# The kernel product of an SSM mixer, computed on quarters of the matrix engine's columns

## The chip, the cores and the metric

The kernel runs on one core of a Trainium2 chip. The metric is the device time of one execution in microseconds, the median of repeated runs. A core has TensorE (PE in the profile, with its weight loads as PEld), VectorE (DVE), ScalarE (ACT), GpSimd (POOL) and SyncE (SP), each with its own instruction stream that it takes in order, and DMA queues.

## The reference

The program is one inference step of a two-layer streaming encoder on 1024 prompt positions and 64 sample positions, 1088 columns in all, width 1024. Layer 0 mixes tokens by windowed attention, layer 1 by a diagonal state-space model (SSM). Each mixer is followed by a gated ConvFFN of inner width 2816. Only the SSM matters here:

```python
def s5_mixer(h, h0_re, h0_im, lam_re, lam_im, log_dt, b_re, b_im, c_re, c_im, d_skip, w_glu, b_glu):
    ...
    lr, li, bbr, bbi = s5_discretize(lam_re, lam_im, log_dt, b_re, b_im)
    ...
        _, _, sr, si = lax.associative_scan(_affine_combine, (ar, ai, xr, xi), axis=1)
        y = jnp.einsum('blgp,gip->blgi', sr, cr) - jnp.einsum('blgp,gip->blgi', si, ci)
    ...
    y = ys.transpose(1, 0, 2, 3, 4).reshape(b, t, D_MODEL) + d_skip.astype(jnp.float32) * h.astype(jnp.float32)
```

There are 64 groups of 16 channels, each with a complex state of 64 dimensions. The parameters do not depend on the activations, so what follows from them alone can be computed at any time before the SSM layer runs.

## The kernel before, in words

The kernel handles eight positions at a time. Within such a block of eight, the output is a product with a short matrix kernel, K[t] = Re(C A^t B) for t = 0 to 7, of 16 by 16 for each group. Between blocks a scan carries the state, for which the kernel needs the tables B A^s and C A^t and some phase tables. All of these are written to a DRAM array `prm`, from which the SSM stage loads them.

**The preparation.** `ssm_prep` (L1098) is a generator that makes the tables as side work while layer 0's ConvFFN runs its up-projection. It first runs `ssm_small` (L892), which makes the discretised parameters with many small VectorE instructions, and then eight chunks, `ssm_chunk(q)` (L1016) and `ssm_toeplitz(q)` (L1086). A chunk has 8 groups, as 4 pairs; the two groups of a pair lie on partitions 0 to 63 and 64 to 127. In the order of the code a chunk does this:

- VectorE builds `ct`, C A^t for t = 0 to 8, real and imaginary (L1034 to L1039, through two scratch tiles `m`). ScalarE copies it, rearranged, to `oc` (L1042), which SyncE's queue stores to `prm` (L1043).
- ScalarE writes B of the 8 groups into the tile `bd` (L1048). `bd` is zeroed once (L1007) and holds, for each pair g and each of real and imaginary c, a matrix of 128 by 128, in which the pair's 32 columns stand at 32 g and all others are zero.
- VectorE builds `w`, B A^s (L882 to L887, the helper `cmul`).
- TensorE multiplies `bd` by `ct` into the PSUM tile `kps` (L1062): eight matmuls, all accumulated over the whole 128 rows, since the zero columns add nothing to the other pairs. They are in float32, which takes two passes each, so the profile shows 16 a chunk.
- VectorE adds D to K[0] and copies `kps` into `kt` (L1066, L1067). SyncE's queue stores `kt` to `kd` (L1068), from which `ssm_toeplitz` reads it back in eight loads as tile `tl` (L1094). ScalarE copies that to `tp` (L1095), which goes to `prm` (L1096).
- TensorE transposes `w` into two PSUM tiles `wps` (L1073), four transposes for the real part (c = 0) and four for the imaginary part (c = 1). ScalarE copies each into `b3` (L1074), which goes to `prm` (L1075).
- GpSimd makes phase tables `tab` (L1081, shown as L882 to L887 on POOL), which its queue stores (L1084).

**Buffers.** `ct`, `oc`, `w`, `b3`, `tab`, `tl` and `tp` share two buffers (`pt`, L136), so a chunk's tiles wait for one another's stores. `m` has one buffer. `kps` and the `wps` of c = 0 share the PSUM buffer `sm0`; the `wps` of c = 1 uses `sm1`.

**What sets the order.** The tile framework writes each engine's instruction order ahead of the run. Each instruction has a priority, which is its place in the order of tracing, and each engine takes the instruction of lowest priority number among those that the framework holds ready. `later(n)` (L118) shifts that number. The up-projection calls `aside` (L443) after every tile of 128 output features, and `aside` advances the preparation by one `yield` with its numbers shifted later by `LOW` = 1500 (L447). So the side work ranks behind the main work around it, and fills what it leaves free. `order(x, behind)` (L112) adds that a matmul of the chunk may not stand ahead of the last up-projection matmul traced before it (L1059).

**The main work around it.** `up_block` (L401) computes one tile of 128 features for one block of columns (384, 384 and 320): 8 steps in the inner dimension times 3 matmuls (`mm3`, L221 to L225: high and low parts of a split float32) into one of six PSUM buffers `mm`. VectorE multiplies each block by the norm's factors (L411, L413) and does two taps of the convolution (L420, L421), the gate (L437), half of the weights' split (L216) and sums for a later product (L358 to L373, tile `jt`).

Elsewhere in the program, attention computes `po` (L796) in two matmul shapes of 64 columns, one for PSUM partitions 0 to 63 and one for 64 to 127, and the norms transpose a row factor on TensorE (L284).

Of the kernel before, what the change touches and what calls it, by code (L numbers as in the profile page):

```python
# [8 lines left out]
F32 = mybir.dt.float32  # L9
F32R = mybir.dt.float32r  # L10
I32 = mybir.dt.int32
AF = mybir.ActivationFunctionType
# [3 lines left out]
P = 128  # L16
# [9 lines left out]
LOW = 1500  # L26
# [17 lines left out]
class Core:  # L44
# [166 lines left out]
    behind = ()  # L211
# [680 lines left out]
    def ssm_small(self):  # L892

        nc, a = self.nc, self.a
# [5 lines left out]
        sm = self.prep.tile([P, 1024], F32, name="sm0", tag="sm").rearrange("p (a q) -> p a q", a=32)  # L900
# [79 lines left out]
        c, s = cs, sn  # L980
        for k in range(10):
# [8 lines left out]
            c, s = (ph[:, 0, k - 2], ph[:, 1, k - 2]) if k > 1 else (ta[:, 8], ta[:, 9])  # L990
# [3 lines left out]
        for t, n, p0 in ((self.tq[:, :, 0:32], 16, 0), (self.tp[:, :, 18:36], 9, 4)):  # L994
            t = t.rearrange("p q (c k) -> p q c k", c=2)
            V.memset(t[:, :, 0, 0:1], 1.0)
            V.memset(t[:, :, 1, 0:1], 0.0)
            w, k = 1, p0
            while w < n:
# [3 lines left out]
                m = [m[:, i, :NPR * u].rearrange("p (q j) -> p q j", j=u) for i in range(2)]  # L1003
                self.cmul(V, [t[:, :, i, w:w + u] for i in range(2)], [t[:, :, i, 0:u] for i in range(2)], y, m)
                w, k = w + u, k + 1
        self.bd_ = self.prep.tile([P, 4, 2, P], F32, name="bd", tag="sm")
        V.memset(self.bd_, 0.0)  # L1007
        self.dv = self.prep.tile([P, 24], F32, name="dv")
        nc.sync.dma_start(self.dv[:, 16:], a["s_d"])
# [6 lines left out]
    def ssm_chunk(self, q):  # L1016

        nc, a = self.nc, self.a
        G, V = nc.gpsimd, nc.vector
        gs = slice(4 * q, 4 * q + 4)  # L1020
# [8 lines left out]
        ct = self.pt([P, 4, 2, 9, 16], "ct")  # L1029
# [13 lines left out]
        nc.sync.dma_start(self.prm[:, gs, OC:OC + 256], oc.rearrange("p g c i t -> p g (c i t)"))  # L1043

        for e, r in enumerate((slice(0, 64), slice(64, 128))):
            o = self.bd_[r, 0, 0, 16 * e:16 * e + 1]
            o = bass.AP(tensor=o.tensor, offset=o.offset, ap=[o.ap[0], [2 * P + 32, 4], [P, 2], [1, 16]])
            nc.scalar.activation(o, self.tq[r, gs, 32:64].rearrange("p g (c j) -> p g c j", c=2), AF.Copy)  # L1048

        w = self.pt([P, 4, 2, 16, 8], "w")  # L1050
        m = self.pm2()
# [5 lines left out]

        kps = self.sm_ps("kps", 0)
        behind = self.last_mm  # L1059
        for g in range(4):  # L1060
            for c in range(2):
                x = nc.tensor.matmul(kps[:, :P], self.bd_[:, g, c], ct[:, g, c, 0:8].rearrange("p t i -> p (t i)"),  # L1062
                                     start=g + c == 0, stop=g + c == 4)
                self.order(x, behind)
        kt = self.prep.tile([P, P], F32, name="kt")
        V.scalar_tensor_tensor(kt[:, 0:16], self.dv[:, :16], self.dv[:, 16 + q:17 + q], kps[:, 0:16], op0=ALU.mult, op1=ALU.add)  # L1066
        V.tensor_copy(kt[:, 16:], kps[:, 16:P])  # L1067
        nc.sync.dma_start(self.kd[q * P:q * P + P, 7:].rearrange("j t i -> j (t i)"), kt)  # L1068
        b3 = self.pt([P, 4, 2, P], "b3")
        for c in range(2):  # L1070
            wps = self.sm_ps("wps", c)
            for g in range(4):
                self.order(nc.tensor.transpose(wps[:, g * P:g * P + P], w[:, g, c].rearrange("p j s -> p (j s)"), self.ident), behind)  # L1073
            nc.scalar.activation(b3[:, :, c], wps.rearrange("p (g n) -> p g n", g=4), AF.Copy)  # L1074
        nc.sync.dma_start(self.prm[:, gs, OW:OW + 256], b3.rearrange("p g c n -> p g (c n)"))  # L1075

# [523 lines left out]
```

## Time and profile before

| | |
|---|---|
| median of 3 runs | 2255.86 us (2252.57 to 2258.36) |
| the profiled execution, its own time | 2264.88 us |
| its span, first to last instruction | 2263.1 us |
| mean granted TensorE clock | 0.990 |
| up-projection of layer 0 with the SSM preparation | about 402 to 925 us of the span |
| chunks of the preparation (L1007 on) | about 590 to 925 us |
| PE busy from 590 to 925 us | 327.78 of 335 us |
| VectorE busy in the same stretch | 251.28 us |

A row of the timeline has the start, the duration, the engine, the line of the kernel, the operation, out<-in by tile names, the shape and the count, and in brackets the engine's idle time before it with what ended that. `128*128` on a matmul is rows by columns of the weights. Matmuls are pipelined, so their durations overlap, and what one costs is read from start to start. The profile names the helper's line where a helper records the operation, as with L882 to L887 for `cmul`.

### The profile page before, as it was taken

How to read it: one execution, taken by the hardware profiler on the slowest of the kernel's cores; microseconds unless marked ns; L12 is line 12 of the kernel's file. 1: busy time of each engine (PE TensorE's matmuls, PEld its weight loads, DVE VectorE, ACT ScalarE, POOL GpSimd, SP SyncE). 2: the span in 40 equal slices, each digit the busy share in tenths (PEclk: the TensorE clock that was granted, in tenths of full speed). 3: DMA queues.
4: the chain of work that ended last, by engine and by line, in shares of the span. 5: the costliest groups of instructions: out<-in, count | busy, mean ns of one | idle time of the engine just before them, and what ended most of it. 6: DMA issues, size and time to landing. Idle time of an engine off the chain costs nothing. (4 is left out here: it accounts for less than half of the span.)

```text
span 2263.1 us, 36074 instructions
## 1 busy us (share of the span) xinstructions
PE 2201.7 (97%) x13875; PEld 2122.4 (94%) x13875; DVE 1688.5 (75%) x2954; ACT 1019.2 (45%) x1839; POOL 415.2 (18%) x474
## 2 busy tenths in 40 slices
PE   8999999999999999999998899999999999999997
PEld 8987789999999999999996799999999999989997
DVE  8677647989877777667767855588997787686764
ACT  5255747422333343455534641263544444355543
POOL 5322004200042423000200034352011011100000
PEclk9999999999999999999998999999999999999999
DMA  5100014656345565887749888652266577578773
GB/s 195 37 21 29 16 65 151 242 191 211 107 138 185 178 203 179 259 288 222 227 164 339 262 286 300 234 166 74 96 233 218 213 287 258 193 250 278 222 256 99
DMA packets 208124, 428.48 MB, mean 189 GB/s; under 512 B 23312, under 2 KB 114224, under 8 KB 205008
## 3 DMA queue, kind: packets, MB, share of 16 engines
q1 hardware_dynamic: 175648, 326.56, 44.0%
q0 software_dynamic: 23984, 95.12, 11.6%
q10 hardware_dynamic: 8320, 4.49, 0.9%
q8 instruction: 109, 1.79, 0.3%
q14 instruction: 63, 0.52, 0.1%
HBM read 297.75 MB, written 128.37 MB: 188 GB/s over the span
## 5 line engine op out<-in xcount | busy, mean ns | idle before, releaser
L223 PE MATMUL mm<-hl,whl 128*128 128x384 f32 (+1 forms) x1960 | 643.8, 329 | 7.7 <-DVE hl L306 3.1
L225 PE MATMUL mm<-hh,whl 128*128 128x384 f32 (+1 forms) x1960 | 641.1, 328 | 2.3 <-DVE whl L216 2.3
L224 PE MATMUL mm<-hh,whl 128*128 128x384 f32 (+1 forms) x1960 | 642.2, 328 | 0.0
L223 PEld LDWEIGHTS mm<-hl,whl 128*128 128x128 f32 x1960 | 368.4, 188 | 10.8 <-DVE hl L306 4.5
L225 PEld LDWEIGHTS mm<-hh,whl 128*128 128x128 f32 x1960 | 368.4, 188 | 2.9 <-DVE whl L216 2.9
L224 PEld LDWEIGHTS mm<-hh,whl 128*128 128x128 f32 x1960 | 368.7, 188 | 0.0
L216 ACT ACTIVATE whl<-raw 128x1024 fp32r<-128x1024 f32 x202 | 212.9, 1058 | 339.1 <-PE mm L225 176.4
L216 DVE TENSOR_TENSOR whl<-raw,whl 128x1024 fp32r<-128x1024 f32 x202 | 254.4, 1263 | 96.7 <-ACT whl L216 96.2
L223 PE MATMUL mm<-gt,whl 128*128 128x384 f32 (+1 forms) x968 | 318.5, 329 | 7.9 <-DVE y L613 3.6
L225 PE MATMUL mm<-gt,whl 128*128 128x384 f32 (+1 forms) x968 | 316.9, 328 | 0.7 <-DVE whl L216 0.7
L224 PE MATMUL mm<-gt,whl 128*128 128x384 f32 (+1 forms) x968 | 317.3, 328 | 0.0
L223 PEld LDWEIGHTS mm<-gt,whl 128*128 128x128 f32 x968 | 182.9, 189 | 10.5 <-DVE y L613 4.9
L225 PEld LDWEIGHTS mm<-gt,whl 128*128 128x128 f32 x968 | 182.7, 189 | 1.0 <-DVE whl L216 1.0
L224 PEld LDWEIGHTS mm<-gt,whl 128*128 128x128 f32 x968 | 182.8, 189 | 0.0
L194 DVE TENSOR_TENSOR whl<-raw,whl 128x1024 fp32r<-128x1024 f32 x84 | 96.3, 1153 | 73.0 <-ACT whl L193 72.4
L193 ACT ACTIVATE whl<-raw 128x1024 fp32r<-128x1024 f32 x84 | 82.6, 986 | 126.8 <-DMA raw<-sd 51.0
L419 ACT ACTIVATE t<-u,ppt 128x1090 f32<-128x1090 f32 x88 | 114.2, 1298 | 50.6 <-DVE u L521 24.6
L420 DVE SCALAR_TENSOR_TENSOR t<-u,ppt,t 128x1090 f32<-128x1090 f32 x88 | 123.6, 1406 | 9.8 <-ACT t L419 9.1
L421 DVE SCALAR_TENSOR_TENSOR t<-u,ppt,t 128x1090 f32<-128x1090 f32 x88 | 123.4, 1403 | 0.4
L563 DVE TENSOR_TENSOR gt<-gr,gt 128x768 fp32r<-128x768 f32 (+2 forms) x106 | 90.2, 880 | 10.7 <-ACT gt L562 10.1
L331 POOL TENSOR_TENSOR y<-y,xl 128x768 f32<-128x768 f32 (+1 forms) x16 | 31.3, 1954 | 354.0 <-DVE y L328 288.0
L562 ACT ACTIVATE gt<-gr 128x768 fp32r<-128x768 f32 (+2 forms) x106 | 78.3, 771 | 39.5 <-DMA gr<-gd 30.2
(390 smaller groups left out, 4181.0 us busy)
## 6 DMA issues: line engine op xcount, KB each, us to landing
raw<-in_w_up SPq DMA_DIRECT2D x88, 512.0 KB, 4.3
raw<-in_w_down SPq DMA_DIRECT2D x74, 512.0 KB, 4.5
raw<-sd SPq DMA_DIRECT2D x40, 512.0 KB, 4.6
sj<-in_w_up POOLq DMA_DIRECT2D x68, 256.0 KB, 6.4
su<-sj POOLq DMA_DIRECT2D x34, 512.0 KB, 5.8
raw<-su SPq DMA_DIRECT2D x34, 512.0 KB, 4.8
pm<-prm SPq DMA_DIRECT2D x32, 522.0 KB, 8.2
gr<-td SPq DMA_DIRECT2D x40, 384.0 KB, 5.9
```

Of the source, the lines that this page charges most:

```text
L193: nc.scalar.activation(w[:, 0], raw, AF.Copy)
L194: nc.vector.tensor_sub(w[:, 1], raw, w[:, 0].bitcast(F32))
L216: x = nc.scalar.activation(w[:, 0], raw, AF.Copy), nc.vector.tensor_sub(w[:, 1], raw, w[:, 0].bitcast(F32))
L223: nc.tensor.matmul(out, w[:, 0, sl], xl, start=start, stop=False)
L224: nc.tensor.matmul(out, w[:, 0, sl], xh, start=False, stop=False)
L225: self.last_mm = nc.tensor.matmul(out, w[:, 1, sl], xh, start=False, stop=stop)
L331: x = by[q].tensor_add(yq, yq, xs[q])
L419: nc.scalar.activation(t, u[:, 0:T + 2], AF.Identity, bias=cb(m), scale=cw(0, m))
L420: nc.vector.scalar_tensor_tensor(t, u[:, 1:T + 3], cw(1, m), t, op0=ALU.mult, op1=ALU.add)
L421: self.last_conv = nc.vector.scalar_tensor_tensor(t, u[:, 2:T + 4], cw(2, m), t, op0=ALU.mult, op1=ALU.add)
L562: nc.scalar.activation(x[:, 0, u], raw, AF.Copy)
L563: nc.vector.tensor_sub(x[:, 1, u], raw, x[:, 0, u].bitcast(F32))
```

## The change

The tile `bd` is cut to the pair's own 32 columns: each of its 8 matrices is now 128 by 32. The eight products go to four different quarters of PSUM partitions, `kps[32 g : 32 g + 32]`, each accumulated over two matmuls (c = 0 and 1) in place of eight. The loops are swapped, so that four successive matmuls go to four different quarters. The products and the transposes get priority numbers that are 4 x 1500 lower than before. The transposes of the imaginary part (c = 1) are traced ahead of those of the real part.

```diff
-        self.bd_ = self.prep.tile([P, 4, 2, P], F32, name="bd", tag="sm")
+        self.bd_ = self.prep.tile([P, 4, 2, 32], F32, name="bd", tag="sm")
...
         for e, r in enumerate((slice(0, 64), slice(64, 128))):
-            o = self.bd_[r, 0, 0, 16 * e:16 * e + 1]
-            o = bass.AP(tensor=o.tensor, offset=o.offset, ap=[o.ap[0], [2 * P + 32, 4], [P, 2], [1, 16]])
-            nc.scalar.activation(o, self.tq[r, gs, 32:64].rearrange("p g (c j) -> p g c j", c=2), AF.Copy)
+            nc.scalar.activation(self.bd_[r, :, :, 16 * e:16 * e + 16], self.tq[r, gs, 32:64].rearrange("p g (c j) -> p g c j", c=2), AF.Copy)
...
-        for g in range(4):
-            for c in range(2):
-                x = nc.tensor.matmul(kps[:, :P], self.bd_[:, g, c], ct[:, g, c, 0:8].rearrange("p t i -> p (t i)"),
-                                     start=g + c == 0, stop=g + c == 4)
+
+        for c in range(2):
+            for g in range(4):
+                with self.later(-4 * LOW):
+                    x = nc.tensor.matmul(kps[32 * g:32 * g + 32, :P], self.bd_[:, g, c], ct[:, g, c, 0:8].rearrange("p t i -> p (t i)"),
+                                         start=c == 0, stop=c == 1)
                 self.order(x, behind)
...
-        for c in range(2):
+        for c in (1, 0):
             wps = self.sm_ps("wps", c)
             for g in range(4):
-                self.order(nc.tensor.transpose(wps[:, g * P:g * P + P], w[:, g, c].rearrange("p j s -> p (j s)"), self.ident), behind)
+                with self.later(-4 * LOW):
+                    x = nc.tensor.transpose(wps[:, g * P:g * P + P], w[:, g, c].rearrange("p j s -> p (j s)"), self.ident)
+                self.order(x, behind)
```

## The prediction

> **What bounds the kernel now.** I read the page first, for the engine with the least idle time.
>
> ```profile
> PE 2201.7 (97%) x13875; PEld 2122.4 (94%) x13875; DVE 1688.5 (75%) x2954; ACT 1019.2 (45%) x1839; POOL 415.2 (18%) x474
> ```
>
> TensorE (PE) is busy 97% of a 2263.1 us span, so a change pays by the PE time or PE idle time that it takes away. The changed lines run between 590 and 925 us, beside the first ConvFFN's up-projection, so next I asked for the waits of PE in that stretch (total, times, longest) and for its groups of instructions (busy, mean ns, idle before).
>
> ```profile
> PE wps L1073 <- DVE kt L1067: 4.4, 3, 1.7
> PE wps L1073 <- DVE w L887: 2.9, 3, 1.2
> ```
>
> ```profile
> L1062 PE MATMUL kps<-ct,bd 128*128 128x128 f32 x128 | 23.8, 272 | 0.0
> ```
>
> These are all the waits of PE there: six, 7.3 us, all ahead of the transposes. In three of them `kt` had not yet been copied out of `kps` (both use PSUM bank sm0), in three `w` was not finished. The products `kps` have no wait. Durations overlap, so costs have to come from start to start, which the timeline of PE gives.
>
> ```profile
> 617.84 0.38 PE L1062 MATMUL kps<-ct,bd 128*128 128x128 f32 x2
> 617.98 0.39 PE L223 MATMUL mm<-hl,whl 128*128 128x320 f32 x1
> 618.21 0.38 PE L1062 MATMUL kps<-ct,bd 128*128 128x128 f32 x2
> 618.35 0.40 PE L224 MATMUL mm<-hh,whl 128*128 128x320 f32 x1
> 618.58 0.31 PE L225 MATMUL mm<-hh,whl 128*128 128x320 f32 x1
> 618.73 0.30 PE L223 MATMUL mm<-hl,whl 128*128 128x320 f32 x1
> 618.87 0.31 PE L224 MATMUL mm<-hh,whl 128*128 128x320 f32 x1
> ```
>
> One `kps` product (two passes, "x2") and one `mm` of the up-projection alternate. A cycle takes 618.21 - 617.84 = 0.37 us; an `mm` alone takes (618.87 - 618.58) / 2 = 0.145. So a product costs 0.225 us, a pass 0.1125, the eight of a chunk 1.8 us, all eight chunks 14.4 us. That is the most the first half of the change can work on.
>
> **The change part by part.** *Quarter columns.* Each product now fills 32 output columns, so four should run abreast. No 32-column product is in this trace; attention's `po` has 64-column ones, in two halves.
>
> ```profile
> 141.06 0.31 PE L225 MATMUL gq<-hh,whl 128*128 128x320 f32 x1
> 141.30 1.09 PE L796 MATMUL po<-ptT,vt 128*64 128x256 f32 x8
> 142.32 0.44 PE L789 MATMUL tps<-ident,ptT 128*128 128x128 f32 x2
> ```
>
> PE was free for `po` at 141.06 + 0.145 = 141.205 and went on at 142.32: 1.11 us for eight passes of 256 columns. One after the other they would take 8 x 0.225 = 1.8; two abreast 0.9. So they ran two abreast, and going into this shape and out of it cost 0.21. For `kps`: 16 passes on four quarters, 4 x 0.1125 + 0.21 = 0.66 us a chunk in place of 1.8, a gain of 1.14, times eight 9.1 us. Bounds: if only two run abreast, as in the row, 0.9 + 0.21 = 1.11 and a gain of 5.5; if none do, 1.8 + 0.21 and a loss of 1.7. I take 9.1, since the row shows full overlap for as many column groups as its work had.
>
> The weight loads of `po` in the same place:
>
> ```profile
> 141.29 0.64 PEld L796 LDWEIGHTS po<-ptT,vt 128*64 128x64 f32 x8 [0.19 <-issue]
> ```
>
> Eight loads lie within 0.64 us, under the matmuls of 141.30 to 142.39. The Trainium skill, TensorE: Matmul & The Clock Gate, Part 3, says that weight loads overlap matmuls in flight only where the row groups differ; quarters of the columns share all rows, so by that rule the loads would lie bare and the gain be lost. This row disagrees for halves; that it holds for quarters is not shown, and it is a rival below.
>
> *In one run, early.* The products and transposes got priority 1500 later than where they are traced, and now 4500 earlier. Before, PE reached them by priority; that is why they alternate with `mm`, whose numbers run beside theirs. Now they go into PE's order as soon as the schedule holds their inputs ready. For the transposes a run saves nothing:
>
> ```profile
> 620.01 0.27 PE L1073 MATMUL wps<-ident,w 128*128 128x128 f32 x1
> ...
> 620.27 0.27 PE L1073 MATMUL wps<-ident,w 128*128 128x128 f32 x1
> ...
> 621.53 0.34 PE L224 MATMUL mm<-hh,whl 128*128 128x384 f32 x1
> 621.71 0.60 PE L1073 MATMUL wps<-ident,w 128*128 128x128 f32 x4
> 622.07 0.42 PE L225 MATMUL mm<-hh,whl 128*128 128x384 f32 x1
> 622.33 0.34 PE L223 MATMUL mm<-hl,whl 128*128 128x384 f32 x1
> ```
>
> Two `mm` of 384 columns (0.175 each, the step from 622.33 back over the run) and four transposes take 0.80 us, so one is 0.1125; an interleaved one, in a cycle of 0.26 us with an `mm` of 0.145, costs 0.115: no difference.
>
> *The old waits.* With c = 1 first, into bank sm1, and the products well ahead of `w`, the copy of `kt` has the whole building of `w` to finish in. The 4.4 us go. The 2.9 us for `w` go as they stand too, and what may come instead is counted as new, below. Each wait also costs a restart:
>
> ```profile
> 779.87 0.34 PE L223 MATMUL mm<-hl,whl 128*128 128x384 f32 x1
> 781.65 0.63 PE L1073 MATMUL wps<-ident,w 128*128 128x128 f32 x4 [1.44 <-DVE kt L1067]
> ```
>
> From 779.87 to 781.65 is 1.78 us where 0.175 would do: 1.6 lost, 0.16 above the idle time. The six waits are worth 7.3 + 6 x 0.16 = 8.2 us.
>
> *The new waits.* This decides the sign. A run that PE meets early makes every `mm` behind it wait for `ct` (L1039) and `w`, because PE takes its instructions in order. Today the products have room:
>
> ```profile
> 801.81 0.76 DVE L1036 TENSOR_TENSOR ct<-m 128x576 f32<-128x576 f32 x1 [5.02 <-ACT tp L1095]
> 802.48 1.35 DVE L421 SCALAR_TENSOR_TENSOR t<-u,ppt,t 128x1090 f32<-128x1090 f32 x1
> 803.75 0.55 DVE L411 TENSOR_TENSOR u<-rb,mm 128x384 f32<-128x384 f32 x1
> ...
> 806.95 0.75 DVE L1039 SCALAR_TENSOR_TENSOR ct<-m 128x576 f32<-128x576 f32 x1
> ```
>
> `ct` was done at 807.70 and PE met `kps` here:
>
> ```profile
> 796.90 0.34 PE L225 MATMUL mm<-hh,whl 128*128 128x384 f32 x1
> ...
> 813.86 0.38 PE L1062 MATMUL kps<-ct,bd 128*128 128x128 f32 x2
> ```
>
> That is 6.2 us of cover, which the early priority gives away. How late the side work really is can be read from VectorE's (DVE's) order. L1036 was written ahead of the L411 at 803.75, which takes the block that PE closed at 796.90 + 0.34 = 797.24 (counting blocks against L411s). A ready L411 outranks side work, so the schedule held L1036 startable by 797.24; on the chip it started at 801.81, 4.6 us later, held by the load of the Toeplitz tile. Over the chunks:
>
> ```profile
> DVE ct L1036 <- ACT tp L1095: 29.9, 7, 6.2
> DVE w L884 <- DMA prm<-oc: 9.6, 7, 2.8
> ```
>
> 29.9 us in seven waits, 4.3 us each. Against that stands what the schedule allows between an input and a matmul placed at its readiness. The broadcast transposes of the norms (L284) are such, with lower-ranking `mm` all around:
>
> ```profile
> 1545.05 0.16 DVE L291 SCALAR_TENSOR_TENSOR nvsqb<-nvsqb 128x3 f32<-128x3 f32 x1
> ```
>
> ```profile
> 1122.47 0.32 PE L284 MATMUL pr<-ident,nvsqa 128*128 128x128 f32 x1 [0.81 <-DVE nvsqa L291]
> ...
> 1548.89 0.49 PE L284 MATMUL pr<-ident,nvsqb 128*128 128x128 f32 x3
> ```
>
> The input was there 1548.89 - 1545.21 = 3.7 us before PE came in one case and 0.8 us after in another. The second figure already contains a late VectorE, so I take 3.0, near the upper end: new waits of 7 x (4.3 - 3.0) = 9.1 us. Ends: zero, and 29.9 if nothing is allowed. The second row above helps a little: `kps` run early frees the buffer of `ct`, so `w` need not wait for the store of `oc`; that is VectorE's time, hidden behind PE, and priced at nothing. The store of `kd` and the copies to `b3` move with their matmuls on SyncE's and ScalarE's queues, in the same order and number; if a weight load queued behind one of them came late, PE would show a wait for `whl`, of which it now has none in this stretch.
>
> *The smaller `bd`.* One memset of 256 elements a partition instead of 1024, once, on VectorE: nothing.
>
> **The sum.** -9.1 - 8.2 + 9.1 = -8.2 us. The profiled execution took 2264.88 us, 9.0 above the median of 2255.86; the change is the same amount in both, so about 2256.7 if profiled, and 2247.7 by the median. A difference under 0.3%, 6.8 us, can't be told from none here.
>
> **The rivals.** *PE takes over the side work's lateness (slower).* Place: the first `kps` of a chunk, waiting for `ct`. Price: 29.9 us of new waits, so -9.1 - 8.2 + 29.9 = +12.6, 2268.5 us. It decides against the change from 17.3 us of new waits, 2.5 us a chunk, that is once the schedule's allowance is under 1.8. For it: the waits of L1036 are there in all seven chunks. Against: the 3.7 us seen at L284.
>
> *The quarters do not run abreast*, by the rule named above or because the runs are broken up by `mm`. Then +1.7 - 8.2 + 9.1 = +2.6, 2258.5 us. For it: no quarter is in the trace. Against: the `po` rows.
>
> *No new waits.* The side chain has fewer waits of its own (9.6 us on L884 go), and the allowance covers the rest: -17.3, 2238.6 us. Against: six waits exist today with 6 us of cover.
>
> **How the numbers follow.** Forecast 0.45 (its own range 2243 to 2254), slower rival 0.20, quarters not abreast 0.15, no new waits 0.20. The forecast's gain of 8.2 lies just over the 6.8 bound, so it gives 0.25 to faster and 0.20 to same; no new waits is all faster; the quarters give 0.12 to same and 0.03 to slower; the slower rival 0.17 to slower, 0.03 to same. Together 0.45 faster, 0.35 same, 0.20 slower. The range goes from 2238, no new waits, to 2268, the slower rival's price; beyond it lie the lower half of the one and the upper half of the other, 2 in 10.
>
> **What would show it.** `kps` as 128*32, sixteen passes within 0.7 us, no `mm` between; if a chunk's run takes 1 us or more the first term is wrong. No idle time at L1073 for `kt`. A new row of PE waiting at L1062 for `ct`: under 10 us in all bears out the forecast, 20 or more the slower rival. Chunks closer together than today, as PE no longer holds them back; now the eight lie within 615.6 to 893.5 us, some 39 apart:
>
> ```profile
> L1062 PE MATMUL kps<-ct,bd x128: 270/273/275, 615.6 to 893.5; 128*128 128x128 f32 x128
> ```
>
> If the run behaves and the waits are gone, yet the time stays, look for PE waits on `whl` or on `u` in the same stretch.

## The result, and the profile after

| | before | after |
|---|---|---|
| median | 2256.61 us (2252.57 to 2258.36, 4 runs) | 2275.2 us (2272.19 to 2279.82, 4 runs) |
| profiled execution, its own time | 2264.88 us | 2273.9 us |
| its span | 2263.1 us | 2272.1 us |
| mean granted clock in it | 0.990 | 0.986 |

The changed kernel is slower by 0.9%: ratio 1.0087, 95% interval 1.0064 to 1.0109, or 18.6 us by the medians. The forecast was 2247.7 us, its range ended at 2268.

Of the page of the changed kernel, the line of busy times (PE had 2201.7 us, DVE 1688.5 before):

```profile
PE 2201.1 (97%) x13875; PEld 2115.9 (93%) x13875; DVE 1689.7 (74%) x2954; ACT 1018.2 (45%) x1839; POOL 421.2 (19%) x474
```

PE executes as many instructions as before and is busy as long, while the span is 9 us longer; so the loss must be idle time, or work at a slower pace. The waits of PE from 590 to 925 us in the changed kernel (total, times, longest), which were six at the transposes before:

```profile
PE kps L1062 <- DVE ct L1036: 15.5, 7, 5.2
```

The six old waits are gone, seven new ones have come at the products, and they are longer. The products in the view by tile (min/median/max of one in ns, then first and last start), and one chunk's products in the timeline of PE:

```profile
L1062 PE MATMUL kps<-ct,bd x128: 272/297/419, 596.6 to 850.2; 128*32 128x128 f32 x128
```

```profile
596.30 0.33 PE L224 MATMUL mm<-hh,whl 128*128 128x384 f32 x1
596.56 0.43 PE L1062 MATMUL kps<-ct,bd 128*32 128x128 f32 x8
596.91 0.44 PE L225 MATMUL mm<-hh,whl 128*128 128x384 f32 x1
597.19 0.33 PE L223 MATMUL mm<-hl,whl 128*128 128x384 f32 x1
...
598.92 0.34 PE L224 MATMUL mm<-hh,whl 128*128 128x384 f32 x1
599.19 0.43 PE L1062 MATMUL kps<-ct,bd 128*32 128x128 f32 x8
599.55 0.44 PE L225 MATMUL mm<-hh,whl 128*128 128x384 f32 x1
599.83 0.34 PE L223 MATMUL mm<-hl,whl 128*128 128x384 f32 x1
```

The quarters do run abreast, but in two runs of four products (eight passes each), with twelve `mm` between in this chunk and 12 to 30 in the others. The first run (c = 0) needs only the real half of `ct` (L1036), the second the imaginary half (L1039), and the schedule put each where its own input was held ready. From 596.30 to 597.19 is 0.89 us in which two `mm` take 0.35; a run costs 0.54, a chunk 1.1 instead of 1.8.

Now the longest of the waits: first PE, then DVE and ACT in the same microseconds of the changed kernel.

```profile
768.51 0.34 PE L223 MATMUL mm<-hl,whl 128*128 128x384 f32 x1
774.03 0.65 PE L1062 MATMUL kps<-ct,bd 128*32 128x128 f32 x8 [5.18 <-DVE ct L1036]
774.62 0.69 PE L224 MATMUL mm<-hh,whl 128*128 128x384 f32 x1
775.10 0.52 PE L225 MATMUL mm<-hh,whl 128*128 128x384 f32 x1
775.42 0.52 PE L223 MATMUL mm<-hl,whl 128*128 128x384 f32 x1
```

```profile
766.23 0.54 DVE L411 TENSOR_TENSOR u<-rb,mm 128x384 f32<-128x384 f32 x1
773.22 0.76 DVE L1036 TENSOR_TENSOR ct<-m 128x576 f32<-128x576 f32 x1 [6.45 <-ACT tp L1097]
```

```profile
771.27 1.92 ACT L1097 ACTIVATE tp<-tl 128x1024 f32<-128x1024 f32 x1 [13.04 <-DMA gd<-t]
```

Three engines stand in a row: PE waits for `ct`, DVE for the copy `tp<-tl` of the chunk before, and that copy came late. The `mm` behind the wait show a second cost: their starts are 0.32 us apart, not 0.174. The stretch cut into pieces of 3.41 us, with the granted clock in the column after the busy times:

```profile
764.48:767.89 3.41, 3.41 (x23) 3.41 (x22) 2.29 (x4) 0.00 (x0) 0.12 (x1) 1.00 0.88 243
767.89:771.30 3.41, 0.96 (x6) 0.64 (x4) 0.00 (x0) 0.03 (x1) 0.00 (x0) 1.00 0.71 218
771.30:774.71 3.41, 0.68 (x9) 0.30 (x9) 1.46 (x3) 2.83 (x2) 0.00 (x0) 0.50 0.18 63
774.71:778.13 3.42, 3.42 (x11) 3.42 (x12) 3.42 (x8) 2.67 (x5) 0.00 (x0) 0.50 1.04 327
778.13:781.54 3.41, 3.41 (x26) 2.96 (x25) 3.41 (x6) 1.57 (x3) 0.00 (x0) 1.00 0.87 299
```

A piece in which PE was idle for most of the time is followed by a piece at half clock: 11 instructions of PE lie in the fourth, 26 in the fifth.

To compare kernels, I measured in each trace the time from one `mm` at 565 us to another, 1960 `mm` later (before: 565.38 to 919.14, 353.8 us; after: 565.23 to 926.08, 360.9), and split it by the steps from start to start: the `mm` themselves (323.9 us in each, at 0.146 or 0.174 apiece), what products and transposes add, waits over 0.15 us, and what the `mm` take longer at half clock. A product or transpose at half clock takes longer too, and that part is in its own column: without it and the restart behind a wait, the changed kernel's products would cost some 8.9 us instead of 9.9 (16 runs of 0.555) and e4's some 6.2 instead of 8.5 (8 runs of 0.773, as in e6). This is called the stretch below; each row is one execution, the ratio is that of the timed runs. (In an edited kernel a line can stand a few numbers off.)

| kernel | stretch | products | transposes | waits | half clock | ratio of times (95%) |
|---|---|---|---|---|---|---|
| before | 353.8 | 14.3 | 8.4 | 7.2 | 0 | |
| before, profiled again (e12) | 349.5 | 14.3 | 7.9 | 3.5 | 0 | 1.000 (0.999 to 1.001) |
| after | 360.9 | 9.9 | 7.1 | 15.5 | 4.4 | 1.0087 (1.0064 to 1.0109) |
| after, old order of halves (e8) | 363.8 | 10.7 | 7.7 | 16.7 | 4.9 | 1.0062 (1.0046 to 1.0078) |
| e1_no_early | 365.2 | 34.1 | 7.1 | 0 | 0 | 1.0068 (1.0048 to 1.0087) |
| e2_early_only | 374.5 | 16.6 | 7.1 | 18.1 | 8.8 | 1.0089 (1.0072 to 1.0106) |
| e3_run_old_place | 353.1 | 10.4 | 8.0 | 7.7 | 3.1 | 1.002 (1.0006 to 1.0033) |
| e4_imag_first | 362.9 | 8.5 | 7.9 | 17.2 | 5.0 | 1.0051 (1.0035 to 1.0067) |
| e5_swap_only | 356.2 | 14.3 | 10.0 | 6.5 | 1.6 | 1.0008 (0.9996 to 1.002) |
| e6_run_late_transposes | 347.2 | 6.2 | 8.4 | 8.9 | 0 | 1.0032 (1.0019 to 1.0046) |
| e9_full_late_transposes | 360.8 | 14.3 | 9.0 | 10.0 | 3.6 | 1.0066 (1.005 to 1.0081) |
| e10_tiling_swap | 349.0 | 6.2 | 9.1 | 8.4 | 1.6 | 1.0016 (1.0006 to 1.0026) |
| e11_tiling_only | 349.8 | 6.2 | 9.6 | 9.5 | 0.6 | 1.0012 (1.0001 to 1.0022) |
| e13_less_dve | 360.4 | 6.2 | 9.5 | 14.7 | 6.0 | 1.0056 (1.0034 to 1.0079) |
| e14_tiling_no_oc | 349.6 | 6.2 | 8.3 | 8.2 | 3.1 | 0.9991 (0.9978 to 1.0004) |
| e15_after_no_oc | 365.9 | 10.6 | 7.4 | 17.2 | 6.8 | 1.006 (1.0037 to 1.0083) |
| e16_before_no_oc | 348.7 | 14.3 | 7.7 | 2.8 | 0 | 0.9967 (0.9953 to 0.9981) |
| e17_tiling_short_tab | 347.1 | 6.2 | 8.9 | 6.9 | 1.2 | 1.0021 (1.0008 to 1.0033) |
| e18_before_short_tab | 346.7 | 14.3 | 7.7 | 0.9 | 0 | 0.9993 (0.998 to 1.0007) |
| e19_after_short_tab | 351.7 | 9.5 | 7.4 | 9.1 | 1.6 | 0.9994 (0.9979 to 1.0009) |

### The profile page after: what moved, and what is told of

Same layout as the page of the kernel before. It is cut to its first block, busy times and chain, and to the rows that moved or that the text cites. A ratio compares the mean times of both kernels' runs of the same rounds, so it can differ in the third digit from the quotient of the medians.

```text
span 2272.1 us, 36102 instructions
## 1 busy us (share of the span) xinstructions
PE 2201.1 (97%) x13875; PEld 2115.9 (93%) x13875; DVE 1689.7 (74%) x2954; ACT 1018.2 (45%) x1839; POOL 421.2 (19%) x474
## 5 line engine op out<-in xcount | busy, mean ns | idle before, releaser
L223 PEld LDWEIGHTS mm<-hl,whl 128*128 128x128 f32 x1960 | 370.2, 189 | 10.6 <-DVE hl L306 5.8
L411 DVE TENSOR_TENSOR u<-rb,mm 128x384 f32<-128x384 f32 (+1 forms) x164 | 80.3, 501 | 31.9 <-PE mm L225 27.1
```

Of the source, the lines that this page charges most:

```text
L223: nc.tensor.matmul(out, w[:, 0, sl], xl, start=start, stop=False)
L411: nc.vector.tensor_mul(u[:, t0 + 2:t0 + 2 + np_], rb[:, t0:t0 + np_], ps[:, :np_])
```

## The experiments

The theories. **P**: the early place makes the loss, since PE, which takes its instructions in order, waits for `ct`. **Q**: the quarter shape makes it. **D**: the stretch isn't where the time hangs; what is gained or lost there changes behind it.

**e1_no_early.** The changed kernel without the priority, products and transposes both.

```diff
-                with self.later(-4 * LOW):
+                if True:
```

> Quarter columns and the other order of the transposes, but the priority of the products and transposes as before. Theory P (the early place makes PE wait for ct): no PE wait for ct at L1062, the 7 us of waits at the transposes stay. But the products stand alone between matmuls of the up-projection, so each pays for going into the quarter shape and out of it. In the changed kernel a run of four products cost 0.55 us, of which 0.23 is passes, so one alone should cost about 0.5 and the 64 of them 32 us in place of 14.4: 2270 to 2278 us. Rival Q (the quarter shape itself is what costs): slower as well, by the same rows. This run prices the shape; it does not tell the two apart.

Measured: 2272.25 us. The waits in the stretch are gone, all of them (P had expected the 7 us at the transposes to stay), and the time is as bad for another reason. The timeline of PE in this kernel:

```profile
615.62 0.34 PE L225 MATMUL mm<-hh,whl 128*128 128x384 f32 x1
615.88 0.41 PE L1062 MATMUL kps<-ct,bd 128*32 128x128 f32 x2
616.22 0.41 PE L223 MATMUL mm<-hl,whl 128*128 128x320 f32 x1
616.57 0.41 PE L1062 MATMUL kps<-ct,bd 128*32 128x128 f32 x2
```

Products and `mm` alternate. A cycle takes 616.57 - 615.88 = 0.69 us, and less 0.145 for the `mm` a product costs 0.54 instead of 0.225: each change of shape is paid for, in both directions. The eight chunks' products cost 34.1 us instead of 14.3. So the quarters need the run, and the early place was the change's way to get it.

**e2_early_only.** The kernel before, full columns and old loops, with the early priority alone.

```diff
+                with self.later(-4 * LOW):
                     x = nc.tensor.matmul(kps[:, :P], ...
...
+                with self.later(-4 * LOW):
                     x = nc.tensor.transpose(wps[:, g * P:g * P + P], ...
```

> Full columns and the old order of the loops; only the early priority of products and transposes is taken over. Theory P: PE waits at L1062 for ct, 10 to 20 us in all, with half clock after the longest waits; the old waits at the transposes go; nothing is gained on the products: 2262 to 2276 us. Rival Q: without the quarter shape there is nothing to lose, and the old waits go: 2246 to 2256 us.

Measured: 2276.17 us. The waits of PE in the stretch:

```profile
PE kps L1063 <- DVE ct L1036: 18.1, 6, 4.6
```

The early place alone costs as much as the whole change: P holds, and Q isn't needed for the loss. (The place is not quite the same: the schedule put e2's products up to 90 `mm` earlier than the changed kernel's.)

**e3_run_old_place.** The changed kernel with the products at the old place, seven of eight in one run, and the transposes about 20 `mm` behind. (The comments in the cuts of code from here on are added for the reader.)

```diff
-                with self.later(-4 * LOW):    # products
+                with self.later(0):
-                with self.later(-4 * LOW):    # transposes
+                with self.later(20):
```

> Quarter columns, products all at one priority number at the old place, so that seven of the eight stand in one run there, transposes 20 numbers later than that. Theory P: no PE wait for ct, few or none at the transposes, the products some 1.1 us a chunk in place of 1.8: 5 to 6 us gained there and up to 8 at the waits: 2242 to 2250 us. Rival Q: the shape costs as in the changed kernel, 2268 or more. Rival D (what is lost comes after 925 us): 2256 or more, with no waits at the products.

Measured: 2261.67 us. The loss is gone but for 0.2%, which speaks for P and against Q; the gain that P expected isn't there. Its waits:

```profile
PE wps L1074 <- DVE kt L1067: 7.7, 5, 3.2
```

**e4_imag_first.** The changed kernel with the imaginary half first, so that the first product already needs all of `ct`.

```diff
-        for c in range(2):
+        for c in (1, 0):
...
-                                         start=c == 0, stop=c == 1)
+                                         start=c == 1, stop=c == 0)
```

> The changed kernel with the imaginary part first among the products, so that the first of them needs all of ct and the eight stand in one run. Theory P: the waits for ct stay, now for L1039, 8 to 20 us in all; one entry and exit less a chunk gains 0.3 us, 2.6 in all: 2266 to 2278 us. Rival Q: half the entries and exits are gone, so the loss against before should halve: near 2266 us, with the waits no matter.

Measured: 2268.29 us. The eight products stand in one run and cost 8.5 us instead of 9.9 (6.2 instead of 8.9 at full clock), the waits stay: 16.2 us for `ct` (L1039) and 1.1 for `kt`. Two runs or one is a small matter beside the waits.

**e5_swap_only** and **e8_after_no_swap**: the kernel before with the transposes' halves in the new order, and the changed kernel with them in the old order.

```diff
-        for c in range(2):
+        for c in (1, 0):
             wps = self.sm_ps("wps", c)
```

> The kernel before with one edit: the two halves of the transposes in the other order. The first four then stand 4 `mm` behind the last product instead of 9, the second four 12 `mm` further on instead of 7, and nothing goes early. Every theory here expects little: the first four are ready at the same moment as before (they need w, which both halves share) and the waits before them in the kernel before were 7.2 us in the stretch from about 565 to 919 us. Theory P (the early place of the products made the loss): 2252 to 2266 us, the wait for w at the transposes up by at most 5 places x 0.17 us x 8 chunks = 7 us. A rival, that the swap by itself carries the loss: 2272 us or more.

> The changed kernel with the transposes' halves in the old order. With all of them put early the order on TensorE, ScalarE, GpSimd and SyncE is the same as in the changed kernel. Theory P: the same time, 2270 to 2279 us, and the same waits for ct (14 to 18 us) in the stretch from about 565 to 919 us, which would be some 6 to 10 us longer than in the kernel before. The rival, that the swap of the halves carries part of the loss: below 2266 us. D (a part of the loss lies behind that stretch): the milestones behind 930 us are later than the kernel before's by more than this stretch has lost.

Measured: 2258.09 and 2270.27 us. The swap does nothing that can be told from none. e8 stands for a second look at the changed kernel, since the order on PE is the same: its waits for `ct` are 16.7 us, its half clock 4.9.

**e12_before_again.** No edit.

> The kernel before, profiled once more, to see how far one profiled execution of it lies from another, stage by stage. If its first profile (8 us above its median) was long in the last stages only, this one has the same 353 to 355 us in the stretch from about 565 to 919 us and is some 8 us shorter behind 1930 us; the loss of the changed kernel is then 7 to 10 us in the stretch and 8 behind it. If the stretch itself varies, it comes out below 348 us, and the whole loss of the changed kernel lies in the stretch.

Measured: 2254.34 us, span 2251.5. The waits of PE in the stretch were shorter by half than in the first profile:

```profile
PE wps L1073 <- DVE kt L1067: 2.8, 3, 1.4
PE wps L1073 <- DVE w L887: 0.6, 1, 0.6
```

The stretch itself varies, by 4.3 us, and what lies behind it by 7.4 (1344.0 and 1336.6 us from the end of the stretch to the end of the span). The expectation's two cases came half each. With two profiles of either order, the stretch is 351.7 us on average before and 362.4 after, 10.7 more; behind it, 1340.3 and 1342.3 (1346.0 and 1338.5), 2 more. That makes 12.7 us, near the 13.2 of e8's runs and below the 18.6 of the first comparison. D isn't needed for the loss: 10.7 of the 12.7 us lie in the stretch. (Of all twenty profiles, e2 and e15 have the longest stretches and the shortest rest, 1330 us; part of such a loss may come back behind the stretch, but both were also the fastest executions of their kernels, so it can be scatter.)

**e6_run_late_transposes** and **e9_full_late_transposes.** All eight products in one run at the old place, the transposes 17 and some 35 `mm` behind: e6 in quarters, e9 over the full columns, in the same order at every place of PE.

```diff
+                with self.later(0 if g + c else 2):    # products
...
+                with self.later(20 if c else 50):      # transposes, c = 1 first
```

> The quarters, all eight products in one run at the old place, the first transposes about 17 `mm` behind them and the second four 16 to 22 further on. Theory P: the products wait for nothing (at that place they waited for nothing in the kernel before and in e3_run_old_place), the transposes stand some 5 places behind those of e3_run_old_place, whose waits for kt were 7.7 us at five of eight, so these go mostly; without waits the clock is not halved. In the stretch from about 565 to 919 us the products cost 5 to 6 us instead of 14.3, the transposes about 8, the waits 0 to 3 instead of 7.2: 11 to 16 us below the kernel before, 2241 to 2250 us. The rival D (anything that is gained in this stretch is lost again downstream of it, as the place of the products is not what the time hangs on): 2255 us or more, with the stretch itself shorter.

> The same order as in e6_run_late_transposes on every place of TensorE, but the products over all 128 columns into a zero-padded square, as before: the price of the quarters alone, in one run each. P: 8 chunks x (1.8 - 0.66) = 9 us slower than e6_run_late_transposes by the prediction's figures, 2250 to 2259 us. If the quarters gain nothing (their switch costs what they save): the same as e6_run_late_transposes within 3 us.

Measured: 2263.01 and 2271.71 us. A chunk's run in e6:

```profile
615.56 0.31 PE L224 MATMUL mm<-hh,whl 128*128 128x320 f32 x1
615.80 0.64 PE L1062 MATMUL kps<-ct,bd 128*32 128x128 f32 x16
616.37 0.41 PE L225 MATMUL mm<-hh,whl 128*128 128x320 f32 x1
```

Its weight loads, and the same chunk's run in e9:

```profile
615.80 0.38 PEld L1062 LDWEIGHTS kps<-ct,bd 128*32 128x32 f32 x16 [0.19 <-issue]
```

```profile
615.83 0.31 PE L224 MATMUL mm<-hh,whl 128*128 128x320 f32 x1
615.97 1.95 PE L1063 MATMUL kps<-ct,bd 128*128 128x128 f32 x16
617.67 0.39 PE L225 MATMUL mm<-hh,whl 128*128 128x320 f32 x1
```

In e6, from 615.56 to 616.37, less an `mm`, is 0.665 us: the prediction's 0.66 for a chunk, with nothing yet for the slower `mm` behind it; with that, 6.2 us for all eight chunks instead of 14.3. In e9 the same stretch of a chunk, 615.83 to 617.67 less an `mm`, is 1.70 us. At equal order the quarters are worth 8.1 us on PE and 8.7 in time (9 expected), so Q is refuted, and with the opposite sign. But e6 as a whole came out 0.3% slower than the kernel before, where P expected a gain. The order of the two is what costs: e9, with the old full columns in this order, is 0.66% slower than the kernel before, more than the quarters bring. Where e6 loses is not settled: its profiled execution, 2255.4 us, was the fastest of its twelve, and its stretch is 4.5 us shorter than the average of before, so the result is what D had forecast (2255 us or more, with the stretch shorter).

**e10_tiling_swap** and **e11_tiling_only.** The quarters in one run at the old place, the transposes where they were within a few `mm`; e10 with the swapped halves, e11 without (its loop is `for c in range(2)` again), which leaves the quarters alone.

```diff
+                with self.later(0 if g + c else 2):    # products
...
+                with self.later(10):                   # transposes
```

> The quarters in one run of eight at the old place, the transposes about where the kernel before has them (11 and 7 `mm` on instead of 9 and 7), with the swapped halves; nothing early. P: in the stretch from about 565 to 919 us the products cost 6.2 us as in e6_run_late_transposes instead of 14.3, the transposes 8 to 10, the waits 6 to 9 us as in the kernel before and e5_swap_only: 344 to 350 us against 353.8. Theory D, by which what this stretch gains is mostly lost again before 1350 us (e6_run_late_transposes: 6.3 us ahead at 891 us, 0.9 us at 1355 us): 2254 to 2260 us, the same as the kernel before. Without D: 2246 to 2252 us.

> As e10_tiling_swap with the transposes' halves in the old order: the quarters in one run and nothing else of the change. The first four now need kt as well as w, 12 `mm` behind the products. P: the same as e10_tiling_swap, plus up to 3 us of waits for kt at the transposes. With D 2254 to 2262 us, without it 2246 to 2254 us.

Measured: 2259.8 and 2259.52 us. The waits of PE in e11:

```profile
PE wps L1074 <- DVE w L887: 6.1, 4, 1.8
PE wps L1074 <- DVE kt L1067: 3.5, 4, 1.4
```

The products cost 8.1 us less, as they should. Against the mean of the two profiles of before, waits (9.5 against 5.4), half clock and transposes (9.6 against 8.2) are 6.1 us more; the stretch is some 2 us shorter, and the time is a little longer. Most of the gain went into waiting for VectorE's side work. Both times lie in the ranges of D. Counted on to a matmul 1800 further behind the stretch, e10 and e11 took 719.0 and 718.4 us from its start, the two profiles of before 722.6 and 715.8: there nothing is left of the gain, though one profile each can't tell a loss behind the stretch from scatter.

**e13_less_dve.** e11 with two of VectorE's instructions ahead of `w` left out.

```diff
-        V.tensor_mul(m1, wide(cr), tall(pi))
-        V.tensor_mul(m2, wide(ci), tall(pr))
-        V.scalar_tensor_tensor(ct[:, :, 1], m1, -1.0, m2, op0=ALU.mult, op1=ALU.subtract)
+        V.tensor_mul(ct[:, :, 1], wide(cr), tall(pi))
```

> e11_tiling_only with two of VectorE's instructions a chunk left out: the imaginary half of ct is one product instead of two products and their difference, so the numbers of the kernel product are others and its time is what counts. That takes 2 x 0.75 = 1.5 us a chunk off the side work ahead of w, 12 us in all; TensorE's work and its order stay. Theory P in its last form (the quarters free 8.1 us on TensorE, and the transposes then wait for VectorE's side work, which sets when w and kt are there): the waits of the stretch fall from 9.5 us to 0 to 2, the clock is not halved in it, and the stretch takes 340 to 343 us instead of 349.8. Rival D (TensorE's own steps set the pace, and the waits are chance): waits of 5 to 10 us, 347 us or more. Behind the stretch the products' chain is as before; in all 2244 to 2254 us by P, 2256 us or more by D.

Measured: 2269.49 us, waits of 14.7. That refutes the theory in this form: it isn't the amount of VectorE's work alone. Its idle time ahead of the first half of `w`, in the groups of VectorE from 590 to 925 us, shows where the 12 us went (e11 had 7.5 there):

```profile
L884 DVE TENSOR_TENSOR w<-m 128x512 f32<-128x512 f32 x8 | 5.5, 692 | 19.7 <-DMA prm<-oc 19.7
```

VectorE had 12 us less to do ahead of this place and waited 12 us longer there, for the store that frees the buffer of `w`; what stands behind that in its queue, `kt` among it, waited too, and all of PE's waits are for `kt`.

**e14_tiling_no_oc, e15_after_no_oc, e16_before_no_oc.** The tile `oc` is left out in e11, in the changed kernel and in the kernel before.

```diff
-        oc = self.pt([P, 4, 2, 16, 8], "oc")
         for c in range(2):
-            nc.scalar.activation(oc[:, :, c], ct[:, :, c, 1:9].rearrange("p g t i -> p g i t"), AF.Copy)
-        nc.sync.dma_start(self.prm[:, gs, OC:OC + 256], oc.rearrange("p g c i t -> p g (c i t)"))
+            nc.sync.dma_start(self.prm[:, gs, OC + P * c:OC + P * c + P], ct[:, :, c, 1:9].rearrange("p g t i -> p g (t i)"))
```

> e11_tiling_only with the staging tile oc left out: the two rearranging copies on ScalarE are not made, ct is stored as it lies, in two stores (so the consumer gets its columns in another order; the amount of work there is the same). w then waits for no store of oc. Theory L (the side work's loop of buffers and stores sets when w and kt are there; the quarters' gain was spent on waiting for it): the waits at the transposes fall from 9.5 us to 0 to 3, the stretch from about 565 to 919 us takes 339 to 344 us instead of 349.8. Rival T (the place is paced by TensorE and VectorE's main work, the waits stay whatever the loop does): 347 us or more.

> The changed kernel with the staging tile oc left out in the same way. The products need only ct, which is made ahead of oc; ct's own start waits for the chunk before. L: the loop of a chunk is shorter by the store's landing (2 to 4 us), so ct is earlier, and the waits for ct fall from 15.5 to 16.7 us to 0 to 8, the stretch from 360.9 to 363.8 us to 340 to 352. If ct's lateness has nothing to do with oc: waits of 13 us or more, 357 us or more.

> The kernel before with the staging tile oc left out in the same way: the yardstick for the other two. Its waits in the stretch (3.5 and 7.2 us in two profiles) fall to 0 to 3 us by L, and the stretch takes 346 to 349 us instead of 349.5 to 353.8; e14_tiling_no_oc is then 6 to 8 us below it, which is what the quarters free on TensorE. By T the two are equal within 3 us.

Measured: 2254.4, 2274.43 and 2250.98 us. The waits of PE in e14, then in e15:

```profile
PE wps L1072 <- DVE kt L1065: 7.6, 5, 2.5
PE wps L1072 <- DVE w L887: 0.5, 1, 0.5
```

```profile
PE kps L1060 <- DVE ct L1036: 17.2, 6, 4.3
```

In e14 the waits for `w` went, as the removed store would have it, and waits for `kt` came in their place. e16 came out as L expected, e14 didn't: the two have the same stretch within 1 us although e14's products cost 8.1 us less. For the quarters alone L is refuted, and T fits. For the early place e15 decides nothing. Without `oc` the schedule put its products up to 128 `mm` earlier than in the changed kernel (by count of the `mm` ahead of them), and on the chip `ct` came earlier as well (L1036 of the last chunk at 833.20 us instead of 845.06); so a shorter side chain and an earlier place stand against one another, and the waits stayed. (e16 is faster than the kernel before by 0.3%, but it leaves ScalarE's copies out, so it isn't a version of the kernel.)

**e17_tiling_short_tab, e18_before_short_tab, e19_after_short_tab.** Four of the six instructions of GpSimd's complex product for `tab` are left out in e11, in the kernel before and in the changed kernel.

```diff
-        m = self.pm2()
-        m = [m[:, i].rearrange("p (g b a) -> p g b a", b=9, a=16) for i in range(2)]
...
-        self.cmul(G, (v(0), v(1)), (wide(ac), wide(as_)), (tall(bc), tall(bs)), m)
+        G.tensor_mul(v(0), wide(ac), tall(bc))
+        G.tensor_mul(v(1), wide(as_), tall(bs))
```

They were chosen from these groups of the changed kernel: GpSimd starts a chunk's `tab` when `w` is done, and VectorE's next chunk then waits for `tab`, whose scratch tile it shares, and for `tp`.

```profile
L1036 DVE TENSOR_TENSOR ct<-m 128x576 f32<-128x576 f32 x8 | 6.1, 758 | 26.4 <-ACT tp L1097 26.4
L1034 DVE TENSOR_TENSOR m<-tq,tp 128x576 f32<-128x576 f32 x8 | 6.0, 753 | 8.9 <-POOL tab L887 8.9
```

```profile
L882 POOL TENSOR_TENSOR m<-tq,tp 128x576 f32<-128x576 f32 x8 | 13.4, 1674 | 344.0 <-DVE w L887 321.0 <-DVE u L393 22.9
```

> e11_tiling_only with GpSimd's complex product for tab cut to two plain products, so four of its six instructions a chunk (about 2 us each, some 8 us a chunk) are left out, and tab no longer shares the scratch tile m with VectorE; the numbers of tab are others. Theory L2 (the loop w, tab, tl, tp, next ct paces the side work, and the quarters' gain was spent on waiting for it): ct's wait for tp falls from 32 us to under 15, the waits at the transposes from 9.5 us to 0 to 3, the stretch from about 565 to 919 us takes 339 to 344 us instead of 349.8. Rival T (whatever the loop does, the waits move elsewhere and the stretch stays): 347 us or more.

> The kernel before with the same four GpSimd instructions a chunk left out: the yardstick. L2: its waits (3.5 and 7.2 us in two profiles) go to 0 to 2 us, the stretch takes 345 to 348 us, so that the quarters alone are 5 to 8 us below it. T: both within 3 us of one another.

> The changed kernel with the same four GpSimd instructions a chunk left out. L2: ct is some 4 to 8 us a chunk earlier, so the early products no longer wait for it, or little (0 to 6 us instead of 15.5 to 16.7), the clock is not halved, and the stretch takes 341 to 350 us instead of 360.9 to 363.8: the early place would then not lose against the kernel before. T: waits of 12 us or more, 356 us or more.

Measured: 2260.63, 2254.61 and 2256.24 us. The waits of PE in e19:

```profile
PE kps L1062 <- DVE ct L1036: 7.7, 3, 3.6
PE kps L1062 <- issue: 1.2, 1, 1.2
PE kps L1062 <- DVE ct L1039: 0.3, 1, 0.3
```

In the changed kernel the waits for `ct` fall by half, the half clock from 4.4 us to 1.6, and the loss is gone: 14 to 19 us for an edit that is worth 2 us, not to be told from none, in the kernel before. (The waits and the stretch stayed a little above what L2 expected.) That is P by its cause: `ct` came up to 16 us earlier than in the changed kernel, and the early place no longer lost, although here too the schedule moved the products forward, by up to 81 `mm`. VectorE's own wait for `tp` ahead of `ct` hardly changed (25.8 us of idle time at L1036 instead of 26.4), so it isn't what measures how late `ct` is for PE. Whether GpSimd's time or the shared scratch tile made `ct` late, this run doesn't tell. For the quarters alone T holds again (e18 came out as L2 expected, e17 didn't): e17 and e18 have the same stretch within 0.4 us, 8.1 us less for products on one side and 8.4 more for waits, half clock and transposes on the other. In e17 VectorE still waits for `tp` ahead of `ct`, 33.7 us, so GpSimd's products weren't what held `tp`.

## Why the prediction was wrong

**The new waits** are the step that failed. The mechanism was the one named: PE takes over part of the 4.3 us by which the side work is late at L1036. The allowance of 3.0 us, read from two rows at L284 and taken near the upper end, was too large. Measured were 15.5 us in seven waits, 2.2 each, so on average the schedule allowed 4.3 - 2.2 = 2.1; e8 gave 16.7, e2 18.1. The term was 9.1.

The term's form, one lateness less one allowance, is too simple as well. VectorE's waits at L1036 in the changed kernel (26.4 us, 3.8 each) and PE's behind them differ by anything from -0.6 to 3.7 us a chunk. In the fourth chunk VectorE waited only 0.70 us there and PE 1.32. In e2's fifth chunk VectorE didn't wait at L1036 at all and PE waited 3.40 us: VectorE came there late from another instruction of its queue, a sum of the main work that had to wait for a load.

```profile
731.70 0.56 DVE L370 TENSOR_TENSOR jt<-jt 128x384 f32<-128x384 f32 x1 [6.89 <-DMA jt<-gd]
```

So what delays VectorE ahead of `ct` makes PE wait too, and the prediction counted only the wait at L1036. One side remark came true: VectorE's wait for the store of `oc` at L884 fell from 11.4 us to 0.9, and it was rightly priced at nothing on PE.

**The half clock** had no place in the sum. The old waits were 0.5 to 1.7 us and cost no clock in the stretch. The new ones go up to 5.2, and what follows runs at half speed: 4.4 us, 4.9 in e8, 8.8 in e2. Waits and clock together are 19.9 us against 9.1, and 17.3 was the point from which the prediction let the slower rival decide. Its mark for telling them apart (under 10 us of waits the forecast, 20 or more the rival) left out this part.

**Quarter columns**, -9.1: the mechanism was right. A run of eight took 0.665 us in e6, but 0.775 with the slower `mm` behind it, which the 0.21 for going in and out had left out; in one run the gain is 8.1. In the changed kernel it failed on "in one run": since the first four products need only L1036, the schedule made two runs, each with its own entry and exit, and the gain was 14.3 - 9.9 = 4.4 (5.4 at full clock). The rival that they don't run abreast is refuted by the row of sixteen passes in 0.64 us, against 1.95 in e9. The Trainium skill, TensorE: Matmul & The Clock Gate, Part 3, says in one sentence that weight loads overlap matmuls in flight only where the row groups differ. Here sixteen loads of quarters of the columns, at least 0.106 us each in the view by tile and so 1.7 us end to end, lie within 0.38 us of that run. The measurement decides.

**The old waits**, -8.2: they went, 7.2 us and 1.3 at the transposes. But they were one execution's; the second profile has 3.5 us of them. The change could save some 5, not 8, and the statement that it is the same amount in any execution was wrong on this term.

The sum with the measured terms, profile against profile: -4.4 - 1.3 - 7.2 + 15.5 + 4.4 = +7.0, against 360.9 - 353.8 = 7.1. Against the average of both profiles of before it is some 2 more, and with e8 10.7.

**Where the forecast's gain would have gone.** At the old place, without the new waits, the -9.1 was not kept either: three pairs (e10 and e11 against before, e14 against e16, e17 against e18) have the products 8.1 us cheaper and the time no better, by the ratios 0.1 to 0.3% longer. PE then waits for `w` or `kt`, which takes most of the gain in the stretch; where the rest and the 0.1 to 0.3% go is not shown, and D stays open for it. Only at an order that is worse by itself did the quarters show in the time (e6 against e9). What paces the side work there is open: it isn't the amount of VectorE's work (e13), the store of `oc` (e14) or GpSimd's products (e17), each by itself. VectorE's idle time ahead of L1036, 23 to 35 us in the twenty traces and most of it put down to `tp`, is the next to look at, with the stores and loads of `kd` and `tl` ahead of it, and so are its waits for the load of `jt` at L370 (18.6 us in the changed kernel). An own buffer for `ct`, which would part it from the chunk before, wasn't tried.

"Chunks closer together" came true (596.6 to 850.2 us, 36 apart instead of 39), and meant nothing: the products were early, the `mm` behind them late.

## What to carry to other kernels

Before putting a step of a side chain early on an in-order engine that is 97% busy, look at what its producer waits for in that place; the scheduler's readiness is a model, and what the producer is later than that model allows stops the main work (15.5 us here), and can cost the clock besides (4.4 us). Shortening the chain took that loss away in e19. Work saved on the busiest engine at a point where it meets a side chain can come back as a wait for the chain: three ways of shortening the chain (e13, e14, e17) didn't bring the saving of the quarters into the time. A term read from waits of one profile needs a second profile before it goes into a sum.

## What the runs showed of the hardware

**The clock.** It is granted in pieces of 3.41 us, and it goes by the idle time of PE in the piece before. In the stretches of all twenty traces of the table, each of the 32 pieces at full clock with 1.89 us idle or more was followed by one at 0.50, and none with less than 1.66 was; of those between, 1.66 to 1.87, four were and eight were not. A piece at half clock took less to be followed by another: the seven with 0.73 us idle or more were, the 36 with 0.36 or less were not. So by these numbers one wait of 2.5 us can cost half of a piece, 1.7 us, more, and four waits of 1.2 us in different pieces at full clock cost no clock. The Trainium skill, TensorE: Matmul & The Clock Gate, Part 1, has a window of 3413 ns and the half clock after at least one idle window; the length agrees with the 3.41 us here, but a window that was idle for a little over half, 1.89 of 3.41 us, was enough.

**Changing the matmul's shape.** Going from 128 to 32 columns and back cost some 0.32 us a run, whether the run had 2 passes (e1: 0.54 a product, 0.225 of it its two passes) or 16 (e6: 0.775, 0.45 of it four sets of passes abreast). Four quarters abreast save that only in a run of several products.
